# The routing table and row fetch of the next expert, moved in front of the down products of the expert before

## The chip, the cores and the metric

One core of a Trainium2 chip runs the whole program. The metric is the device time of one execution in microseconds (us), as the median of three runs.

## What is computed

One decoder layer over 512 tokens of width 2048: a mixer (pooling branch, forgetting attention, gates, output projection), then a mixture of 16 experts, then a last norm. Only the experts matter here:

```python
logits = h @ w_router                      # (512, 16)
# best group of 4 experts, then the 2 best experts in it: two experts per token, with weights
for each expert e, over the rows (at most 128 in a block) of the tokens that chose it:
    a, u = xb @ w_g[e], xb @ w_u[e]        # 2048 -> 1024 each
    y    = (silu(a) * u) @ w_d[e]          # 1024 -> 2048
    x[token] += gate_m * weight * y
```

All is float32. The kernel keeps that precision by splitting an operand into a high and a low part that TensorE reads at its fast rate (`chi` and `clo` of the weights, `xh` and `xl` of the rows, `glp` for both parts of the gated rows), and by adding three products: high by high, low by high, high by low.

## The kernel before

**Steps.** The expert stage is a list of items, one for each 128 rows of a weight matrix. Expert e has 16 gate-and-up steps `gu[e][0..15]` (`gu_item`, its 2048 columns are gate and up side by side) and 8 down steps `dn[e][0..7]` (`d_item`). A step is a load by SP, a split (ScalarE copies the high part, line 1132, then VectorE subtracts to get the low part, line 1133), and 12 matmuls of 512 columns (`rows3`, line 1147): three products into four PSUM banks. Even experts use banks 0 to 3 and odd ones banks 4 to 7 (`cset`).

**Order.** It is written out by hand. The first four gate-and-up steps of the next expert stand ahead of the down steps of an expert:

```python
NCR, LSC, LEAD = 8, 2, 4
c_items += nxt[:LEAD] + dn[e] + nxt[LEAD:]
```

So the list reads gu[e][0..3], dn[e-1][0..7], gu[e][4..15], gu[e+1][0..3], dn[e][0..7] and so on. Every engine works its own queue in this order. `run_items` (line 78) splits two items ahead of the matmuls (LSC), and there are LSC + 1 = 3 pairs of `chi` and `clo`, so the split of a step writes the pair that the step three places earlier has read. What is hung on an item by `.after` is written into the queues just ahead of the matmuls of the next item.

**Work hung on the steps.** After gu[e][15], `glu(e)`: ScalarE's silu (line 1250) and VectorE's product (line 1251) take the gate and up sums out of the four banks into `glr`. After gu[e+1][1], `glu_turn(e)`: TensorE turns these rows into the first two banks of the set (line 1262), and ScalarE and VectorE take them out as `glp` (lines 1267, 1268). After dn[e][7], `put_out(e)`: VectorE scales the down sums into `y` (line 1275, one instruction for each bank), and POOL adds `y` to the rows of the output by an indirect DMA (line 1280).

**Routing of the next expert.** `slot_hits(e)` (line 1575, VectorE) makes a one-hot tile that says which token sits in which of the 128 slots. It lies in the tile `G`. `table(e)` (line 1578) multiplies it on TensorE with a small list (line 1581: four matmuls of 8 columns into one bank), and three short VectorE instructions (lines 1584, 1585, 1588) read that bank and give the token numbers `dest` and the scales `tab`. `gather(e)` (line 1213, POOL) then fetches the expert's rows from DRAM (`zrows`) by an indirect DMA into `G`. `prep_rows` (line 1223, VectorE) scales `G` in four quarters after gu[e-1][9] to gu[e-1][11], and `prep_turn` turns it on TensorE (line 1238) and splits it into `xh` and `xl` (lines 1243, 1244).

Before the change, for expert e+1, the one-hot tile is made after dn[e-1][4], and the table and the fetch follow gu[e][5], which is the second gate-and-up step behind the down steps of expert e-1. The table's bank is the second of the set of expert e+1, which is also the set of e-1.

Of the kernel before, what the change touches and what calls it, by code (L numbers as in the profile page):

```python
# [138 lines left out]
def trunk_kernel(ctx: ExitStack, tc: tile.TileContext, x, c, w_ada, b_ada, norm_mix, norm_moe, w_in,  # L139
# [88 lines left out]
    def bank(i):  # L228
        return psB.tile([P, 512], F32, name=f"bank{i}", tag=f"bank{i}")
# [341 lines left out]
    for g in range(2, 8):  # L571
        n = f"A{g+1}" if g < 7 else "S0"
# [526 lines left out]
    NCR, LSC, LEAD = 8, 2, 4  # L1099
# [7 lines left out]
    def c_tile(name, shape, dt=F32, bufs=1):  # L1107
        return c_["left"].tile(shape, dt, name=name, tag=name, bufs=bufs)
# [102 lines left out]
    def slot_rows(tensor, e, to):  # L1211

        gp.indirect_dma_start(out=to, out_offset=None, in_=tensor[:],
                              in_offset=bass.IndirectOffsetOnAxis(ap=r_["dest"][:, e:e + 1], axis=0),
                              bounds_check=T - 1, oob_is_err=False)

    def gather(e):
        g = got[e] = xs[e] = c_tile("G", [P, D]) if e else xs[0]
        slot_rows(zrows, e, g)
# [118 lines left out]
    gu = {e: [gu_item(e, k) for k in range(KD)] for e in range(E)}  # L1338
    dn = {e: [d_item(e, k) for k in range(8)] for e in range(E)}
# [53 lines left out]
    def rtile(name, n=NBE, dt=F32, bufs=1):  # L1393
        return rt.tile([P, n], dt, name=name, tag=name, bufs=bufs)

    def b_e(t):
        return t.rearrange("p (b e) -> p b e", e=E)
# [7 lines left out]
    vv = v4.rearrange("p (b e c) -> p b e c", e=E, c=4)  # L1405
# [144 lines left out]
    vb = wr.rearrange("p k e -> p (k e)").bitcast(BF16).rearrange("p (b e c) -> p b e c", e=E, c=8)  # L1550
# [15 lines left out]
    ohs = {}  # L1566

    def slot_hits(e):

        oh = rtile("oh", NB * P) if e < 2 else c_tile("G", [P, D])[:, 0:NB * P]  # L1570
        if e:
            oh = oh.bitcast(BF16)[:, 0:NB * P]
        ohs[e] = oh = oh.rearrange("p (b s) -> p b s", b=NB)
        slot, pos = (slotb, posb) if e else (slot1, posm)
        dve.tensor_tensor(oh, slot[:, None, :].to_broadcast([P, NB, P]),
                          b_e(pos)[:, :, e:e + 1].to_broadcast([P, NB, P]), ALU.is_equal)

    def table(e):
        ps, oh, v, n = bank(4 * (e % 2) + 1), ohs.pop(e), vb if e else vv, 8 if e else 4
        for b in range(NB):  # L1580
            pe.matmul(ps[:, 0:n], lhsT=oh[:, b, :], rhs=v[:, b, e, :], start=b == 0, stop=b == NB - 1)
        if e:

            dve.tensor_reduce(at_[:, 0:1], ps[:, 0:2], axis=AX.X, op=ALU.add)
            dve.tensor_reduce(tab[:, e, :], ps[:, 2:8].rearrange("p (c i) -> p c i", i=3), axis=AX.X, op=ALU.add)
        else:
            dve.tensor_copy(tab[:, e, :], ps[:, 1:3])
        dve.tensor_scalar(dest[:, e:e + 1], at_[:, 0:1] if e else ps[:, 0:1], float(T), None, op0=ALU.add)
# [81 lines left out]
    slot_hits(0)  # L1670
    filled()
    table(0)
    gather(0)
    placed()
# [12 lines left out]
    c_items[1:1] = [Item(None, prep_first)]  # L1687
    c_items.insert(5, Item(gu[0][0].raw))
    for e in range(E - 1):
        (dn[e - 1][4] if e else gu[0][2]).after.append(lambda e=e: slot_hits(e + 1))  # L1690
        gu[e][LEAD + 1].after.append(lambda e=e: table(e + 1))
        gu[e][LEAD + 1].after.append(lambda e=e: gather(e + 1))
        for q in range(4):
            gu[e][NORM[q]].after.append(lambda e=e, q=q: prep_rows(e + 1, got[e + 1], q))
            gu[e][TURN[q]].after.append(lambda e=e, q=q: prep_turn(e + 1, q))
# [31 lines left out]
```

## Time and profile before

| | us |
|---|---|
| median of 3 runs | 2397.55 (2397.06 to 2399.11) |
| the profiled execution, its own time | 2397.21 |
| its span in the trace | 2395.5 |
| TensorE busy in the span | 2325.1 (97%) |
| VectorE busy in the span | 1748.3 (73%) |
| ScalarE busy in the span | 1163.7 (49%) |

The expert stage fills the second half of the span, from about 1250 us on. The sections on rows below are read like this: a row of a timeline gives the start, the duration (of all instructions of the row), the engine, the line, the operation with what it writes and reads, and in brackets how long the engine had been idle just before and what ended that. TensorE's matmuls overlap, so the distance from one start to the next is what a matmul costs, and it is shorter than the duration shown.

### The profile page before, as it was taken

What the parts mean: (1) busy time and instruction counts of PE and PEld (TensorE: products, weight loads), DVE (VectorE), ACT (ScalarE), POOL (GpSimd) and SP (SyncE); (2) the same over time, 40 slices, a digit from 0 to 9 for tenths busy, and PEclk for the clock granted to TensorE, in tenths of its full rate; (3) what the DMA queues carried; (4) which work ended last, traced back from release to release, by engine and by line L of the source; (5) the groups of instructions that cost most, each with busy time, mean ns of one, the idle gap of its engine ahead of it and who ended that gap; (6) DMA issues with size and microseconds to landing.
All of it is one profiled execution on the core that took longest, in us unless ns stands there. A gap on an engine that the chain in (4) does not pass through costs nothing.

```text
span 2395.5 us, 29296 instructions
## 1 busy us (share of the span) xinstructions
PE 2325.1 (97%) x11478; PEld 1929.4 (81%) x11478; DVE 1748.3 (73%) x1750; ACT 1163.7 (49%) x1070; POOL 127.7 (5%) x73
## 2 busy tenths in 40 slices
PE   7999999999999999999969999999999999999996
PEld 6888777788887888899968888888788888888883
DVE  7987333377665666343349999999999999999995
ACT  4323323322222222233227777777776777777775
POOL 0000100000000000000000111001101100100010
PEclk9999999999999999999979999999999999999998
DMA  9878724266665667366648999999998999999996
GB/s 338 277 245 205 101 71 71 71 234 240 237 233 192 236 233 256 108 201 196 222 152 314 347 372 384 399 384 368 371 381 345 376 411 366 372 378 376 376 359 264
DMA packets 269775, 662.57 MB, mean 277 GB/s; under 512 B 20084, under 2 KB 160620, under 8 KB 249708
## 3 DMA queue, kind: packets, MB, share of 16 engines
q1 hardware_dynamic: 262112, 641.89, 73.6%
q0 software_dynamic: 4752, 17.48, 3.0%
q8 instruction: 91, 1.49, 0.2%
q10 hardware_dynamic: 2768, 1.29, 0.2%
q14 instruction: 52, 0.43, 0.0%
HBM read 648.32 MB, written 29.39 MB: 283 GB/s over the span
## 4 chain that ended last, share of the span: by engine, by line
PE 77%; DMA 11%; DVE 7%; issue 3%; ACT 2%; POOL 0%; SPq 0%; POOLq 0%; DVEq 0%; ACTq 0%
PE bank L1147 27%; PE bank L242 10%; PE bank L244 10%; PE bank L243 10%; DMA G<-zrows,dest 4%; DVE clo L1133 3%; PE bank L645 3%; PE bank L647 3%; PE bank L648 3%; DMA craw<-in_w_exp_gate_dram 2%; DMA craw<-in_w_exp_down_dram 2%; DVE y L1275 1%; PE bank L1238 1%; ACT chi L1132 1%; PE bank L386 1%
## 5 line engine op out<-in xcount | busy, mean ns | idle before, releaser
L1133 DVE TENSOR_TENSOR clo<-craw,chi 128x2048 fp32r<-128x2048 f32 x270 | 615.7, 2289 | 53.4 <-ACT chi L1132 51.1
L1132 ACT ACTIVATE chi<-craw 128x2048 fp32r<-128x2048 f32 x270 | 518.0, 1920 | 218.3 <-PE bank L1147 202.2
L238 DVE TENSOR_TENSOR wlo<-raw,whi 128x1024 fp32r<-128x1024 f32 (+2 forms) x180 | 213.3, 1185 | 421.4 <-ACT whi L237 387.5
L237 ACT ACTIVATE whi<-raw 128x1024 fp32r<-128x1024 f32 (+2 forms) x180 | 184.6, 1027 | 653.6 <-PE bank L243 356.3
L242 PE MATMUL bank<-hh,whi 128*128 128x512 f32 x846 | 335.5, 397 | 1.4 <-ACT hh L406 1.3
L244 PE MATMUL bank<-hh,wlo 128*128 128x512 f32 x846 | 330.8, 391 | 1.6 <-DVE wlo L238 1.6
L243 PE MATMUL bank<-hl,whi 128*128 128x512 f32 x846 | 330.3, 390 | 0.3 <-DVE hl L410 0.3
L1147 PE MATMUL bank<-chi,xh 128*128 128x512 f32 x1020 | 288.4, 397 | 0.0
L1147 PE MATMUL bank<-clo,xh 128*128 128x512 f32 x1020 | 280.9, 389 | 0.1
L1147 PE MATMUL bank<-chi,xl 128*128 128x512 f32 x1020 | 280.7, 389 | 0.0
L1147 PE MATMUL bank<-chi,glp 128*128 128x512 f32 x992 | 255.4, 389 | 0.3 <-DVE glp L1268 0.3
L1147 PEld LDWEIGHTS bank<-clo,xh 128*128 128x128 f32 x1020 | 191.4, 188 | 41.1 <-DVE clo L1133 0.5
L1147 PEld LDWEIGHTS bank<-chi,xl 128*128 128x128 f32 x1020 | 191.5, 188 | 40.3
L1147 PEld LDWEIGHTS bank<-chi,glp 128*128 128x128 f32 x992 | 186.1, 188 | 39.6 <-DVE glp L1268 0.9
L1147 PEld LDWEIGHTS bank<-chi,xh 128*128 128x128 f32 x1020 | 185.7, 188 | 34.4
L244 PEld LDWEIGHTS bank<-hh,wlo 128*128 128x128 f32 x846 | 159.2, 188 | 36.7 <-DVE wlo L238 3.1
L242 PEld LDWEIGHTS bank<-hh,whi 128*128 128x128 f32 x846 | 159.4, 188 | 35.3 <-ACT hh L406 1.5
L243 PEld LDWEIGHTS bank<-hl,whi 128*128 128x128 f32 x846 | 159.4, 188 | 33.4 <-issue 1.0
L906 DVE SCALAR_TENSOR_TENSOR acc<-raw,cact,acc 128x1024 f32<-128x1024 f32 x120 | 154.0, 1283 | 11.1 <-DMA raw<-in_w_ada_dram 8.5
L645 PE MATMUL bank<-whi,hh 128*128 128x256 f32 x512 | 146.0, 285 | 0.0
L647 PE MATMUL bank<-wlo,hh 128*128 128x256 f32 x512 | 144.8, 283 | 0.0
L648 PE MATMUL bank<-whi,hl 128*128 128x256 f32 x512 | 144.8, 283 | 0.0
(393 smaller groups left out, 3218.5 us busy)
## 6 DMA issues: line engine op xcount, KB each, us to landing
craw<-in_w_exp_down_dram SPq DMA_DIRECT2D x114, 1024.0 KB, 13.3
raw<-in_w_ada_dram SPq DMA_DIRECT2D x82, 1024.0 KB, 6.1
craw<-in_w_exp_gate_dram SPq DMA_DIRECT2D x161, 512.0 KB, 9.9
craw<-in_w_exp_up_dram SPq DMA_DIRECT2D x161, 512.0 KB, 10.0
raw<-in_w_gate_dram SPq DMA_DIRECT2D x32, 1024.0 KB, 5.7
raw<-in_w_branch_dram SPq DMA_DIRECT2D x16, 1024.0 KB, 5.0
raw<-in_w_out_dram SPq DMA_DIRECT2D x16, 1024.0 KB, 9.3
raw<-in_w_in_dram SPq DMA_DIRECT2D x14, 1024.0 KB, 10.7
```

What stands on the lines that cost most here:

```text
L237: act.activation(hi[:, :n], raw[:, :n], AF.Copy)
L238: dve.tensor_tensor(lo[:, :n], raw[:, :n], hi[:, :n].bitcast(F32), ALU.subtract)
L242: pe.matmul(o, lhsT=whi, rhs=xhi, start=first, stop=False)
L243: pe.matmul(o, lhsT=whi, rhs=xlo, start=False, stop=False)
L244: pe.matmul(o, lhsT=wlo, rhs=xhi, start=False, stop=last)
L645: pe.matmul(o, lhsT=sh, rhs=hi[:, js], start=k + kk == 0 and b % 2 == 0, stop=False, skip_group_check=True)
L647: pe.matmul(o, lhsT=sh, rhs=lo[:, js], start=False, stop=False, skip_group_check=True)
L648: pe.matmul(o, lhsT=sl, rhs=hi[:, js], start=False, stop=k + kk == nk - 1, skip_group_check=True)
L906: dve.scalar_tensor_tensor(cell["a"], r, s, cell["a"], op0=ALU.mult, op1=ALU.add)
L1132: act.activation(hi, raw, AF.Copy)
L1133: dve.tensor_tensor(lo, raw, hi.bitcast(F32), ALU.subtract)
L1147: pe.matmul(ps.tiles[n], lhsT=rows, rhs=w[:, n * 512:(n + 1) * 512], start=first and i == 0, stop=last and i == 2)
```

## The change

For every expert from the third on (e+1 with e from 1 to 14), the table and the fetch now follow gu[e][2], so they stand ahead of gu[e][3] and of the eight down steps of expert e-1, eleven items earlier. The one-hot tile follows gu[e-1][15], right behind `glu`, nine items earlier. The table's bank is the fourth of its set and no longer the second, since `glu_turn` uses the first two at that place. For the second expert (e = 0) place and order stay; only the bank is another.

```diff
-        ps, oh, v, n = bank(4 * (e % 2) + 1), ohs.pop(e), vb if e else vv, 8 if e else 4
+        ps, oh, v, n = bank(4 * (e % 2) + 3), ohs.pop(e), vb if e else vv, 8 if e else 4
...
     for e in range(E - 1):
-        (dn[e - 1][4] if e else gu[0][2]).after.append(lambda e=e: slot_hits(e + 1))
-        gu[e][LEAD + 1].after.append(lambda e=e: table(e + 1))
-        gu[e][LEAD + 1].after.append(lambda e=e: gather(e + 1))
+
+        (gu[e - 1][15] if e else gu[0][2]).after.append(lambda e=e: slot_hits(e + 1))
+        at_step = gu[e][LEAD - 2 if e else LEAD + 1].after
+        at_step += [lambda e=e: table(e + 1), lambda e=e: gather(e + 1)]
```

What this does to the queues is shown for one expert in the middle of the stage. Its gate-and-up steps use banks 0 to 3, and the down steps of the expert before use banks 4 to 7.

**Place 1, TensorE, where the down steps begin.** Before, the last high-by-low product of gu[e][3] (`xl`) is followed by the first product of dn[e-1][0] (`glp`); a wait in brackets names the engine waited for:

```order
L1147 MATMUL bank3_12044<-chi1_12063,xl0_11938 128x512
L1147 MATMUL bank4_12141<-chi2_12081,glp_12089 128x512 [waits DVE_49]
L1147 MATMUL bank5_12142<-chi2_12081,glp_12089 128x512 [waits DVE_49]
L1147 MATMUL bank6_12143<-chi2_12081,glp_12089 128x512
L1147 MATMUL bank7_12144<-chi2_12081,glp_12089 128x512
L1147 MATMUL bank4_12141<-clo2_12082,glp_12089 128x512
```

Now the table stands one step earlier on TensorE, between gu[e][2] and gu[e][3], and writes bank 7:

```order
L1147 MATMUL bank3_12046<-chi0_12032,xl0_11938 128x512
L1581 LDWEIGHTS G_12041 [waits DVE_49]
L1581 MATMUL bank7_12125<-wr_82,G_12041 128x8
L1581 LDWEIGHTS G_12041
L1581 MATMUL bank7_12125<-wr_82,G_12041 128x8
L1581 LDWEIGHTS G_12041
L1581 MATMUL bank7_12125<-wr_82,G_12041 128x8
L1581 LDWEIGHTS G_12041
L1581 MATMUL bank7_12125<-wr_82,G_12041 128x8
L1147 MATMUL bank0_12043<-chi1_12065,xh0_11937 128x512 [waits Activation_49]
```

After the 12 matmuls of gu[e][3], dn[e-1][0] begins as before, but its matmul into bank 7 has waits of its own:

```order
L1147 MATMUL bank3_12046<-chi1_12065,xl0_11938 128x512
L1147 MATMUL bank4_12155<-chi2_12083,glp_12091 128x512 [waits DVE_49]
L1147 MATMUL bank5_12156<-chi2_12083,glp_12091 128x512 [waits DVE_49]
L1147 MATMUL bank6_12157<-chi2_12083,glp_12091 128x512
L1147 MATMUL bank7_12158<-chi2_12083,glp_12091 128x512 [waits DVE_49,PE_49]
L1147 MATMUL bank4_12155<-clo2_12084,glp_12091 128x512
```

What moved: the table's four matmuls came in front of gu[e][3], and the fourth matmul of the first down step, which waited for nothing new before, now waits for VectorE and for TensorE's own table in the same bank.

**Place 2, VectorE, at the same place of the program.** Before, between `glu` (`glr`) and the second down step; `clo1` with `craw2` belongs to gu[e][3], `clo2` with `craw3` to dn[e-1][0], `clo0` with `craw0` to dn[e-1][1]:

```order
L1251 TENSOR_TENSOR glr_12036<-bank7_11527,glr_12036 128x512 [waits PE_49,Activation_49]
L1133 TENSOR_TENSOR clo1_12064<-craw2_7013,chi1_12063 128x2048 [waits DMAHW2_49,DMAHW1_49,Activation_49]
L1133 TENSOR_TENSOR clo2_12082<-craw3_7195,chi2_12081 128x2048 [waits DMAHW3_49,Activation_49]
L1268 TENSOR_TENSOR glp_12089<-bank4_12085,glp_12089 128x512 [waits Activation_49]
L1268 TENSOR_TENSOR glp_12089<-bank5_12086,glp_12089 128x512 [waits Activation_49]
L1133 TENSOR_TENSOR clo0_12120<-craw0_6635,chi0_12119 128x2048 [waits DMAHW4_49,Activation_49]
L1133 TENSOR_TENSOR clo1_12138<-craw4_7394,chi1_12137 128x2048 [waits DMAHW5_49,Activation_49]
```

Now:

```order
L1251 TENSOR_TENSOR glr_12036<-bank7_11529,glr_12036 128x512 [waits PE_49,Activation_49]
L1575 TENSOR_TENSOR G_12041<-bT_75,cntw_83 128x512
L1133 TENSOR_TENSOR clo1_12066<-craw2_7013,chi1_12065 128x2048 [waits DMAHW2_49,DMAHW1_49,Activation_49]
L1133 TENSOR_TENSOR clo2_12084<-craw3_7195,chi2_12083 128x2048 [waits DMAHW3_49,Activation_49]
L1268 TENSOR_TENSOR glp_12091<-bank4_12087,glp_12091 128x512 [waits Activation_49]
L1268 TENSOR_TENSOR glp_12091<-bank5_12088,glp_12091 128x512 [waits Activation_49]
L1133 TENSOR_TENSOR clo0_12122<-craw0_6635,chi0_12121 128x2048 [waits DMAHW4_49,Activation_49]
L1584 TENSOR_REDUCE cntw_83<-bank7_12125 128x1 [waits PE_49]
L1585 TENSOR_REDUCE tab_8533<-bank7_12125 128x2
L1588 TENSOR_SCALAR dest_8534<-cntw_83 128x1 [waits DVE_49]
L1133 TENSOR_TENSOR clo1_12152<-craw4_7394,chi1_12151 128x2048 [waits DMAHW5_49,Activation_49]
```

What moved: the one-hot instruction (line 1575) came in behind `glr`, and the three table instructions came in behind the low part of the second down step.

**Place 3, TensorE, where the table stood.** Before, between gu[e][5] and gu[e][6], into the bank that VectorE's second `y` instruction had to leave first:

```order
L1147 MATMUL bank3_12044<-chi2_12268,xl0_11938 128x512
L1581 LDWEIGHTS G_12236
L1581 MATMUL bank5_12336<-wr_82,G_12236 128x8 [waits DVE_49]
L1581 LDWEIGHTS G_12236
L1581 MATMUL bank5_12336<-wr_82,G_12236 128x8
L1581 LDWEIGHTS G_12236
L1581 MATMUL bank5_12336<-wr_82,G_12236 128x8
L1581 LDWEIGHTS G_12236
L1581 MATMUL bank5_12336<-wr_82,G_12236 128x8
L1147 MATMUL bank0_12041<-chi0_12284,xh0_11937 128x512 [waits Activation_49]
```

Now the steps follow each other there:

```order
L1147 MATMUL bank3_12046<-chi2_12280,xl0_11938 128x512
L1147 MATMUL bank0_12043<-chi0_12296,xh0_11937 128x512 [waits Activation_49]
L1147 MATMUL bank2_12045<-chi0_12296,xh0_11937 128x512
L1147 MATMUL bank1_12044<-chi0_12296,xh0_11937 128x512
L1147 MATMUL bank3_12046<-chi0_12296,xh0_11937 128x512
```

What moved: the four table matmuls and their wait for VectorE are gone from here. On POOL the fetch of expert e+1 is now issued ahead of the scatter of expert e-1, and before it was issued behind it. SP's queue has the same loads in the same order.

## Rows read from the trace of the kernel before

**Rows 1.** The page's busy times (engine, busy us and share, instructions) and its chain that ended last by engine.

```profile
PE 2325.1 (97%) x11478; PEld 1929.4 (81%) x11478; DVE 1748.3 (73%) x1750; ACT 1163.7 (49%) x1070; POOL 127.7 (5%) x73
...
PE 77%; DMA 11%; DVE 7%; issue 3%; ACT 2%; POOL 0%; SPq 0%; POOLq 0%; DVEq 0%; ACTq 0%
```

**Rows 2.** The windows view of the stretch of the middle experts: its length, then busy us (and instructions) of PE, PEld, DVE, ACT and POOL, then TensorE's granted clock, the share of the DMA engines, and GB/s.

```profile
1344.00:2248.00 904.00, 893.59 (x4113) 734.15 (x4113) 842.92 (x574) 648.47 (x417) 89.74 (x26) 1.00 0.95 376
```

**Rows 3.** The waits of TensorE from 1300 to 2330 us, all of them: who waited for whom, us in total, times, longest.

```profile
PE bank L1238 <- DVE G L1223: 7.4, 10, 1.5
PE bank L1581 <- DVE y L1275: 3.0, 14, 0.2
```

**Rows 4.** TensorE's timeline: tables (line 1581) of the first, two following and the last of the 14 experts from the third on, and the first turn of `G` (line 1238) behind each of the two in the middle.

```profile
1344.39 0.24 PE L1581 MATMUL bank<-wr,G 128*128 128x8 bf16 x4 [0.22 <-DVE y L1275]
...
1623.29 0.24 PE L1581 MATMUL bank<-wr,G 128*128 128x8 bf16 x4 [0.22 <-DVE y L1275]
1639.82 0.60 PE L1238 MATMUL bank<-ident,G 128*128 128x128 f32 x4
1691.92 0.24 PE L1581 MATMUL bank<-wr,G 128*128 128x8 bf16 x4 [0.21 <-DVE y L1275]
1710.12 0.66 PE L1238 MATMUL bank<-ident,G 128*128 128x128 f32 x4 [1.51 <-DVE G L1223]
...
2247.92 0.24 PE L1581 MATMUL bank<-wr,G 128*128 128x8 bf16 x4 [0.21 <-DVE y L1275]
```

**Rows 5.** TensorE's timeline, the start of the step ahead of a table and of the step behind it: first for the table of the second expert, then for one of those with the wait.

```profile
1272.79 1.07 PE L1147 MATMUL bank<-chi,xh 128*128 128x512 f32 x4
1275.63 1.16 PE L1147 MATMUL bank<-chi,xh 128*128 128x512 f32 x4
...
1688.83 1.07 PE L1147 MATMUL bank<-chi,xh 128*128 128x512 f32 x4
1692.02 1.17 PE L1147 MATMUL bank<-chi,xh 128*128 128x512 f32 x4
```

**Rows 6.** TensorE's timeline where the down steps begin: the first matmuls of dn[e-1][0] (`glp`) for the first two of the 14 experts, for one in the middle with gu[e][3] ahead of it, and for the last of the 14.

```profile
1316.57 1.29 PE L1147 MATMUL bank<-chi,glp 128*128 128x512 f32 x4
...
1386.46 1.07 PE L1147 MATMUL bank<-chi,glp 128*128 128x512 f32 x4
...
1661.63 1.07 PE L1147 MATMUL bank<-chi,xh 128*128 128x512 f32 x4
1664.35 1.07 PE L1147 MATMUL bank<-chi,glp 128*128 128x512 f32 x4
1665.25 1.07 PE L1147 MATMUL bank<-clo,glp 128*128 128x512 f32 x4
...
2220.35 1.07 PE L1147 MATMUL bank<-chi,glp 128*128 128x512 f32 x4
```

**Rows 7.** VectorE's timeline at the same four places. In the middle: `glr`, the low parts of gu[e][3] and dn[e-1][0] in one row, `glp`, the low part of dn[e-1][1]. The other rows are the low part of dn[e-1][1] of the other three.

```profile
1316.76 2.28 DVE L1133 TENSOR_TENSOR clo<-nf,chi 128x2048 fp32r<-128x2048 f32 x1
...
1385.97 2.28 DVE L1133 TENSOR_TENSOR clo<-nf,chi 128x2048 fp32r<-128x2048 f32 x1
...
1656.99 1.28 DVE L1251 TENSOR_TENSOR glr<-bank,glr 128x512 f32<-128x512 f32 x2
1658.18 4.48 DVE L1133 TENSOR_TENSOR clo<-craw,chi 128x2048 fp32r<-128x2048 f32 x2
1662.59 1.28 DVE L1268 TENSOR_TENSOR glp<-bank,glp 128x512 fp32r<-128x512 f32 x2
1663.79 2.29 DVE L1133 TENSOR_TENSOR clo<-craw,chi 128x2048 fp32r<-128x2048 f32 x1
...
2219.78 2.28 DVE L1133 TENSOR_TENSOR clo<-craw,chi 128x2048 fp32r<-128x2048 f32 x1
```

**Rows 8.** VectorE's timeline: a low part with two table instructions behind it, and a one-hot instruction with the low part behind it.

```profile
1626.66 2.29 DVE L1133 TENSOR_TENSOR clo<-craw,chi 128x2048 fp32r<-128x2048 f32 x1
1628.87 0.15 DVE L1584 TENSOR_REDUCE cntw<-bank 128x1 f32<-128x2 f32 x1
1628.93 0.15 DVE L1585 TENSOR_REDUCE tab<-bank 128x2 f32<-128x6 f32 x1
...
1682.31 0.68 DVE L1575 TENSOR_TENSOR G<-bT,cntw 128x512 bf16<-128x512 bf16 x1
1682.91 2.29 DVE L1133 TENSOR_TENSOR clo<-xh,chi 128x2048 fp32r<-128x2048 f32 x1
```

**Rows 9.** ScalarE's timeline: the high part of dn[e-1][1] at the middle place of Rows 6 and 7.

```profile
1661.83 1.92 ACT L1132 ACTIVATE chi<-craw 128x2048 fp32r<-128x2048 f32 x1 [0.72 <-PE bank L1147]
```

**Rows 10.** POOL's timeline at one expert, a scatter and the fetch behind it, and VectorE's first instruction on the fetched rows.

```profile
1693.47 5.58 POOL L1280 DMA_INDIRECT acc<-y,dest  x1 [61.09 <-DVE y L1275]
1699.35 1.66 POOL L1213 DMA_INDIRECT G<-zrows,dest  x1 [0.31 <-issue]
...
1709.32 0.75 DVE L1223 SCALAR_TENSOR_TENSOR G<-G,tab,shrow 128x512 f32<-128x512 f32 x1 [1.85 <-DMA G<-zrows,dest]
```

**Rows 11.** The page's queue of software DMAs (packets, MB, share of 16 engines), and the two longest waits of SP's queue from 1345 to 2250 us.

```profile
q0 software_dynamic: 4752, 17.48, 3.0%
...
SPq L1154 <- DMA acc<-y,dest: 195.0, 14, 15.0
SPq L1185 <- DVE clo L1133: 162.3, 54, 5.8
```

## The prediction

> **What bounds the kernel now.** I read the page first, for the engine that sets the end: TensorE is busy 97% of the span, and 77% of the chain that ended last runs over it [rows 1]. Then the windows view of the expert stage: in 904.0 us TensorE is busy 893.6 us at a granted clock of 1.00, which is its upper level of 2.4 GHz [rows 2]. Third, what TensorE waits for there: two things, and the change touches both, the rows `G` of the next expert (10 waits, 7.4 us) and, ahead of the table, VectorE's `y` (14 waits, 3.0 us) [rows 3]. Last, the timelines, since these lists count idle time from the end of a matmul, while the next one starts before that end. I price by starts.
>
> From table to table is one expert. Thirteen of them take 2247.92 - 1344.39 = 903.53 us, 69.50 each [rows 4]. One without a wait for `G` takes 1691.92 - 1623.29 = 68.63 us [rows 4]. In it the first turn of `G` starts 16.53 us behind the table; in the next one, with a listed wait of 1.51 us, it starts 18.20 us behind, 1.67 us more [rows 4]. The rows are late because of POOL's order: the scatter is issued at 1693.47, the fetch only behind it at 1699.35, and VectorE stands idle for 1.85 us until the rows land [rows 10].
>
> **What the change takes away.** *The wait for `G`.* The fetch is now issued about eleven steps earlier, at 2.72 us a step (1664.35 - 1661.63) [rows 6] some 30 us. The longest loss seen is under 2 us, so I take it as gone: 13 x (69.50 - 68.63) = **11.3 us**. Its low end is the listed 7.4 us [rows 3].
>
> *The table's wait for `y`.* The table of the second expert, which does not wait, costs 1275.63 - 1272.79 - 2.72 = 0.12 us; one that waits for `y` costs 1692.02 - 1688.83 - 2.72 = 0.47 us [rows 5]. At its new place its bank was emptied by `glu` before, and the one-hot tile is ready two steps ahead. So 14 x 0.35 = **4.9 us** go; low end the listed 3.0 [rows 3].
>
> Here a rule bears on the price. By the wait list the two gains are 10.4 us, by starts 16.2. The Trainium skill (Perfetto Trace Analysis, Tensor Engine Instruction) says that the end of a TensorE instruction in a profile is worked out from its size and not observed. By it the list, which rests on such ends, is no price, and the trace agrees: 1.67 us lost against 1.51 listed. With the list's values the sum below would be +13.7, with the starts it is +7.9.
>
> **What it adds.** The table now writes the fourth bank of the set that the down steps of expert e-1 fill next. The fourth matmul of the first down step can't start until VectorE has read the table out (lines 1584 and 1585), and on VectorE these two stand behind the low part of the *second* down step. So TensorE waits for work that it needs only a step later. For the expert in the middle:
>
> - TensorE reaches that matmul at 1664.35 + 0.12 (the table, now ahead of it) + 3 x 0.225 (four matmuls take 1665.25 - 1664.35) = 1665.15 [rows 5, 6].
> - VectorE runs without a gap from `glr` to the low part of dn[e-1][1], which starts at 1663.79 [rows 7]. The one-hot instruction now stands in this train and pushes it by 1682.91 - 1682.31 = 0.60 [rows 8]: 1664.39. Line 1585 starts 1628.93 - 1626.66 = 2.27 behind the start of the low part and takes 0.15 [rows 8], so it ends at 1666.81. From the end of a VectorE instruction to TensorE's start I take 0.05 (1709.32 + 0.75 to 1710.12) [rows 4, 10]: 1666.86.
> - The wait is 1666.86 - 1665.15 = 1.71 us.
>
> The last of the 14 reads alike: the low part starts 0.57 us ahead of the first `glp` matmul, against 0.56 in the middle; the second has 0.49 [rows 6, 7]. Only the first differs, it starts 0.19 us behind [rows 6, 7]; the same sum gives 2.46 us with the push and 1.86 without; I take 1.86. Together 13 x 1.71 + 1.86 = **24.1 us**. Nothing covers it: apart from the two waits above TensorE waits for nothing in this stage, and behind the place it goes on step by step.
>
> Low end: the one-hot's 0.60 us cost nothing. Then 1.11 us stay, since ScalarE starts the high part of dn[e-1][1] at 1661.83, when TensorE has left that buffer, and ends at 1663.75, 0.04 ahead of the low part [rows 7, 9]. 14 x 1.11 = 15.5. High end: all at the second expert's distance (0.07 more), and release only after the third table instruction (line 1588, at most 0.15 more): 14 x 1.93 = 27.0.
>
> **Small moves.** The one-hot leaves the down steps and the three table instructions leave gu[e][5], where VectorE has slack: it is busy 843 of 904 us [rows 2]. The low parts of gu[e][3] and dn[e-1][0] now end at 1661.1 and 1663.3, still 1.6 and 2.1 us ahead of the matmuls that read them [rows 6, 7]; `glp` ends at 1664.47, and its second half is needed at 1664.70. On POOL the fetch goes ahead of the scatter: 30 us apart, neither holds the other up. SP's loads keep their order. I cost these at nothing.
>
> **Sum.** 24.1 - 11.3 - 4.9 = +7.9 us on the profiled execution's 2397.2, that is **2405.1 us**; the median shown is 0.35 above that execution. With 0.2% (4.8 us) as what a measurement of this kernel can tell from no change, this is slower. Ends: 15.5 - 16.2 = -0.7 (2396.5) and 27.0 - 10.4 = +16.6 (2413.8).
>
> **The rivals.**
> 1. *Faster: TensorE does not wait at the fourth matmul.* If VectorE ran far enough ahead there, only the gains stay: 2397.2 - 16.2 = 2381. It decides at (16.2 - 4.8) / 14 = 0.81 us of wait: below that the change is faster. For it: VectorE loses its idle time for `G`, 1.85 us in one expert [rows 10]. Against it: the high part on ScalarE can't start before TensorE has left the buffer [rows 9], which alone gives 1.11. Chance 0.08.
> 2. *No change: the one-hot's push is swallowed.* The low end above, 2396.5. Against it: VectorE shows no gap there [rows 7]. Chance 0.08.
> 3. *No change: the weight loads set the pace.* The DMA engines are 0.95 busy at 376 GB/s [rows 2]. Then moving waits about on TensorE gives 2397. Against it: TensorE waits for no load there [rows 3], and SP's queue waits 162.3 us for tiles that VectorE has yet to free [rows 11], so loads are ahead of their use. The Trainium skill (HBM Reference, Specifications) gives about 358 GB/s for each core; by that the stage's 340 MB would take an estimated 949 us, and the trace ran it in 904, so that figure does not bind here. Chance 0.10.
> 4. *Much slower: the fetch comes between the weight loads.* Queue 0 moved 17.48 MB [rows 11] in 33 transfers (16 fetches, 15 scatters and two at the end of the program), 0.53 MB each, 1.41 us at 376 GB/s [rows 2]. If the loads were late by that each time: 14 x 1.41 = 20 more, 2425. Against it: the same queue of SP as in 3, and its 14 stops of up to 15.0 us for the scatter [rows 11] that no step feels. Chance 0.06.
>
> That the change does not do what it says is no case: the order shows table, wait and fetch at the new places.
>
> **How the numbers follow.** The forecast, 2402 to 2414, has 0.68. With rival 4 slower has 0.74; rivals 2 and 3 make same 0.18; faster 0.08. The range goes from 2396 (rivals 2 and 3) to 2413, just under the high end, and leaves out rivals 1 and 4 and a little at its edges.
>
> **What would show it.** Table to table about 70.0 us (68.63 - 0.35 + 1.71) and nearly equal in all experts. Rows 3 replaced by one wait of TensorE's line 1147 for VectorE's table, 14 times, about 1.55 us each as listed. No wait for `G`, the table's start right behind its step, the fetch issued about 40 us ahead of its first reader. It is wrong if the fourth `glp` matmul follows the third without a gap, if the gap is near 1.1, or if loads show up as TensorE's waits.

## The result, and the profile after

| | before | after |
|---|---|---|
| median of the runs, us | 2397.31 (2396.65 to 2399.11, 4 runs) | 2412.37 (2410.29 to 2413.11, 4 runs) |
| ratio to before, with its 95% interval | | 1.0062 [1.0049, 1.0074] |
| span of the profiled execution, us | 2395.5 | 2411.4 |

The change makes the kernel slower by 15.1 us. The forecast was +7.9 (2405.1, range 2396 to 2413). A second comparison, on another chip, gave 2409.83 and 1.0072 [1.0055, 1.009]; it is told with the experiments.

The page of the changed kernel, busy times and the chain that ended last, as in [rows 1]:

```profile
PE 2326.1 (96%) x11478; PEld 1925.0 (80%) x11478; DVE 1747.1 (72%) x1750; ACT 1163.3 (48%) x1070; POOL 185.4 (8%) x73
...
PE 66%; DVE 16%; DMA 9%; issue 6%; ACT 3%; POOLq 0%; DVEq 0%; SPq 0%; ACTq 0%
```

TensorE does the same work in the same busy time. What is new is idle time between its instructions, and VectorE's share of the chain, which went from 7 to 16%. The windows view from the first to the last of the 14 tables (columns as in [rows 2]):

```profile
1312.38:2229.26 916.88, 895.43 (x4109) 732.37 (x4108) 841.36 (x573) 647.84 (x417) 140.83 (x26) 1.00 0.92 367
```

Thirteen experts take 916.88 us, 70.53 each, where before they took 69.50 [rows 4]. The clock is at its upper level, 1.00, in both. The loads run at 367 GB/s and no longer at 376, as about the same bytes (336 MB against 340) are spread over a longer time. POOL's row grew from 89.74 to 140.83 us; the last section comes back to it.

The wait lists of the changed kernel: TensorE's matmuls from 1300 to 2345 us, all of them (as [rows 3]), then two rows of its weight loads from 1345 to 2265 us.

```profile
PE bank L1147 <- DVE dest L1588: 21.5, 14, 1.6
...
PEld bank L1147 <- issue: 25.0, 13, 1.9
PEld bank L1147 <- DVE clo L1133: 6.9, 13, 0.5
```

Both lines of [rows 3] are gone. In their place stands one wait for the table, 14 times, 1.54 us each as listed. The first row of the weight loads is the same stop once more, seen from the load of the matmul that waits. The last row is easily passed over, since it stands with the weight loads: 13 times TensorE waits for a low part (`clo`), 0.53 us each. It turns out to be the point the prediction missed.

TensorE's timeline, in order of time: the first table; then one expert in the middle from the turn of `glr` on, through the table, gu[e][3] and the first down step; then the start of gu[e][4], and gu[e][7] with its three products; the first turn of `G`; the next turn of `glr` and the next table; and the last table. It answers to [rows 4 to 6].

```profile
1312.38 0.26 PE L1581 MATMUL bank<-wr,G 128*128 128x8 bf16 x4
...
1661.47 1.03 PE L1262 MATMUL bank<-ident,glr 128*128 128x128 f32 x8
...
1665.08 0.26 PE L1581 MATMUL bank<-wr,G 128*128 128x8 bf16 x4
1665.19 1.18 PE L1147 MATMUL bank<-chi,xh 128*128 128x512 f32 x4
...
1668.05 0.84 PE L1147 MATMUL bank<-chi,glp 128*128 128x512 f32 x3
1670.41 0.47 PE L1147 MATMUL bank<-chi,glp 128*128 128x512 f32 x1 [1.52 <-DVE dest L1588]
1670.72 1.09 PE L1147 MATMUL bank<-clo,glp 128*128 128x512 f32 x4
...
1691.60 1.07 PE L1147 MATMUL bank<-chi,xh 128*128 128x512 f32 x4
...
1699.76 1.07 PE L1147 MATMUL bank<-chi,xh 128*128 128x512 f32 x4
1700.93 1.20 PE L1147 MATMUL bank<-clo,xh 128*128 128x512 f32 x4
1701.96 1.07 PE L1147 MATMUL bank<-chi,xl 128*128 128x512 f32 x4
...
1713.76 0.60 PE L1238 MATMUL bank<-ident,G 128*128 128x128 f32 x4
...
1731.95 1.03 PE L1262 MATMUL bank<-ident,glr 128*128 128x128 f32 x8
1735.56 0.26 PE L1581 MATMUL bank<-wr,G 128*128 128x8 bf16 x4
...
2229.26 0.26 PE L1581 MATMUL bank<-wr,G 128*128 128x8 bf16 x4
```

Two things are to be seen. The first down step has three matmuls, then a hole: the fourth should start 3 x 0.225 behind the first, at 1668.73, and starts at 1670.41, **1.68 us** late. And in gu[e][7] the second product starts 1.17 us behind the first and the third 1.03 behind that, where a product takes 0.91 (four matmuls of some 0.225). The turn of `G` waits for nothing.

VectorE at the same place (as [rows 7, 8]), and then where gu[e][7] is prepared:

```profile
1661.62 0.70 DVE L1575 TENSOR_TENSOR G<-bT,cntw 128x512 bf16<-128x512 bf16 x1
1662.22 4.50 DVE L1133 TENSOR_TENSOR clo<-craw,chi 128x2048 fp32r<-128x2048 f32 x2
1666.63 1.30 DVE L1268 TENSOR_TENSOR glp<-bank,glp 128x512 fp32r<-128x512 f32 x2
1667.82 2.30 DVE L1133 TENSOR_TENSOR clo<-craw,chi 128x2048 fp32r<-128x2048 f32 x1
1670.02 0.17 DVE L1584 TENSOR_REDUCE cntw<-bank 128x1 f32<-128x2 f32 x1
1670.09 0.17 DVE L1585 TENSOR_REDUCE tab<-bank 128x2 f32<-128x6 f32 x1
1670.23 0.15 DVE L1588 TENSOR_SCALAR dest<-cntw 128x1 int32<-128x1 f32 x1
...
1695.96 2.72 DVE L1275 SCALAR_TENSOR_TENSOR y<-bank,tab,gmrow 128x512 f32<-128x512 f32 x4
1698.59 2.28 DVE L1133 TENSOR_TENSOR clo<-glr,chi 128x2048 fp32r<-128x2048 f32 x1
```

The table's sums were in the bank from about 1665.3 on. VectorE comes to them at 1670.02, behind the one-hot tile, two low parts, `glp` and the low part of the second down step. It ends line 1588 at 1670.38, and TensorE starts at 1670.41. (Only lines 1584 and 1585 read the bank, and they are done by 1670.26; why TensorE goes on only behind line 1588 was not tested.) Further down, the low part for gu[e][7] (its weights were loaded into the tile `glr`, which is free then) can start only when `y` is done, at 1698.59; it ends at 1700.87, and the product that reads it starts at 1700.93.

**Where the time went.** I cut each expert at four starts on TensorE's timeline, from one turn of `glr` to the next, and added up the 14 experts (us):

| | before | after | difference |
|---|---|---|---|
| turn of `glr` to the first down step (the table's new place) | 88.75 | 92.11 | +3.36 |
| the eight down steps | 304.88 | 330.01 | +25.13 |
| gu[e][4] to the first turn of `G` (the table's old place) | 321.84 | 310.52 | -11.32 |
| first turn of `G` to the next turn of `glr` | 257.13 | 254.73 | -2.40 |
| all | 972.60 | 987.37 | +14.77 |

That is the 15.1 us between the medians, to 0.3. In before, an expert without a wait for `G` takes 22.35 in the third row and 18.20 in the fourth, so these waits made 321.84 - 14 x 22.35 + 257.13 - 14 x 18.20 = 8.9 + 2.3 = 11.3 us. After, all 14 experts read nearly alike: 6.58, 23.56, 22.17 and 18.20, together 70.5.

### The profile page after: what moved, and what is told of

Read it like the earlier page. It is cut to its first block, busy times and chain, and to the rows that moved or that the text cites. A ratio compares the mean times of both kernels' runs of the same rounds, so it can differ in the third digit from the quotient of the medians.

```text
span 2411.4 us, 29297 instructions
## 1 busy us (share of the span) xinstructions
PE 2326.1 (96%) x11478; PEld 1925.0 (80%) x11478; DVE 1747.1 (72%) x1750; ACT 1163.3 (48%) x1070; POOL 185.4 (8%) x73
## 4 chain that ended last, share of the span: by engine, by line
PE 66%; DVE 16%; DMA 9%; issue 6%; ACT 3%; POOLq 0%; DVEq 0%; SPq 0%; ACTq 0%
PE bank L1147 19%; PE bank L244 10%; PE bank L242 10%; PE bank L243 10%; DVE clo L1133 9%; PE bank L645 3%; PE bank L647 3%; PE bank L648 3%; DMA craw<-in_w_exp_down_dram 2%; ACT chi L1132 2%; DMA craw<-in_w_exp_gate_dram 2%; DMA craw<-in_w_exp_up_dram 2%; DVE y L1275 1%; DMA raw<-in_w_gate_dram 1%; DVE G L1223 1%
## 5 line engine op out<-in xcount | busy, mean ns | idle before, releaser
L1147 PE MATMUL bank<-chi,glp 128*128 128x512 f32 x992 | 258.6, 390 | 22.4 <-DVE dest L1588 21.5
L1280 POOL DMA_INDIRECT acc<-y,dest x15 | 123.3, 8219 | 414.8 <-DVE y L1275 414.8
## 6 DMA issues: line engine op xcount, KB each, us to landing
raw<-in_w_in_dram SPq DMA_DIRECT2D x14, 1024.0 KB, 10.4
```

The lines of the kernel that those rows point to most:

```text
L1147: pe.matmul(ps.tiles[n], lhsT=rows, rhs=w[:, n * 512:(n + 1) * 512], start=first and i == 0, stop=last and i == 2)
L1280: gp.indirect_dma_start(out=acc[:], out_offset=bass.IndirectOffsetOnAxis(ap=r_["dest"][:, e:e + 1], axis=0), in_=weigh(e), in_offset=None, ...
```

## The experiments

The theories that the expectations speak of: **A**, the prediction's own, is that the loss is the table's bank, which VectorE empties late because the table instructions stand behind the low part of the second down step. Its rival **B** is that the early fetch or the moved one-hot slows the down steps, and the table's wait only shows it. **G** is on the waits for `G` in the kernel before: that they come from the fetch standing behind the scatter on POOL. Kernels compared on one chip share the runs of before there. These lie between 2385 and 2398 us (one to ten waits for `G` were seen in kernels that leave the fetch at its old place), so each kernel has its own ratio. The names in brackets are those that the expectations may use.

**1. The table one step earlier still (e1).** In the change:

```diff
-        at_step = gu[e][LEAD - 2 if e else LEAD + 1].after
+        at_step = gu[e][LEAD - 3 if e else LEAD + 1].after
```

Expected: 

> The change with table and fetch one step earlier still, behind gu[e][1] and the turn of glr, so that the three table instructions stand ahead of the low part of dn[e-1][1] on VectorE. Theory A (the loss is TensorE waiting at the fourth matmul of the first down step, 1.68 us and 0.11 us of refill, 14 times): the wait vanishes, VectorE leaves the bank at about the time glp ends plus 0.36, some 0.4 us ahead of the fourth matmul. 2412.4 - 14 x 1.79 = 2387.3, plus up to 0.1 us each where the table waits for the one-hot tile (1.4): 2387 to 2389, faster than before by 8 to 10. Theory B (the early fetch, with POOL busy 185 us instead of 128 and the scatter landing after 16.9 us instead of 12.5, slows loads and the stage): the fetch is as early here, so the time stays within 5 us of 2412, or falls by less than half of 25.

Measured: 2386.05 (2383.51 to 2390.0) against 2390.0 for before, ratio 0.9987 [0.9975, 0.9999]. TensorE's timeline of this kernel, the first two products of the first down step and the start of gu[e][4]:

```profile
1659.10 1.07 PE L1147 MATMUL bank<-chi,glp 128*128 128x512 f32 x4
1660.00 1.07 PE L1147 MATMUL bank<-clo,glp 128*128 128x512 f32 x4
...
1680.86 1.07 PE L1147 MATMUL bank<-chi,xh 128*128 128x512 f32 x4
```

The hole is gone, and the eight steps take 21.76 us, as before. In the sum of the 14 experts the down steps went from 330.01 to 304.67 and nothing else moved by over 0.2 us. Fetch and one-hot are at least as early here, and the down steps take no longer for it. A holds, B falls. It also says that the change's whole loss hung on one step's place. The time is a little below the 2387 to 2389 that were expected, but it is 4 us faster than before and not 8 to 10, since before itself takes 2390 on this chip and not 2397.

**2. The first down step bank by bank (e2).** The table stays where the change put it, but the first down step does all three products of one bank before the next, so the table's bank comes up at the tenth matmul and not at the fourth:

```diff
-    def rows3(ps, sh, sl, hi, lo, first, last, order=(0, 1, 2, 3)):
+    def rows3(ps, sh, sl, hi, lo, first, last, order=(0, 1, 2, 3), by_bank=False):
...
-        steps = [(n, i) for n in order for i in range(3)] if last else [(n, i) for i in range(3) for n in order]
+        steps = [(n, i) for n in order for i in range(3)] if last or by_bank else [(n, i) for i in range(3) for n in order]
...
-            rows3(sets[e], gh[:, k, :], gl[:, k, :], *cell.pop("w"), k == 0, k == 7)
+            rows3(sets[e], gh[:, k, :], gl[:, k, :], *cell.pop("w"), k == 0, k == 7, by_bank=k == 0)
```

Expected: 

> The change as it is, but the first down step of each expert runs its 12 matmuls bank by bank, so that the table's bank comes as the 10th matmul and not as the 4th. No instruction is added or moved on another engine. Theory A: TensorE comes to that bank 6 x 0.227 = 1.36 us later, so of the wait of 1.68 us some 0.32 stay: 2412.4 - 14 x 1.36 = 2393.3 (2391 to 2395). Theory B: nothing moves on the queues of DMAs, 2412.

Measured: 2392.68 (2389.23 to 2395.11), ratio 1.0013 [1.0002, 1.0025]. TensorE's waits:

```profile
PE bank L1147 <- DVE dest L1588: 2.1, 12, 0.3
```

The time is in the expected range. The down steps take 310.96 us, 6.1 over those of before, 0.44 an expert where 0.32 was expected: a hole of 0.31 (1663.63 + 0.23 to 1664.17 in its timeline), and again some 0.12 behind it. Six matmuls of 0.225 us put between the table and its reader (1.35 us) took 1.36 out of the 1.80: the loss is a distance in time.

**3. The one-hot tile alone (e5).** In the kernel before, only the one-hot tile goes to its new place:

```diff
-            (dn[e - 1][4] if e else gu[0][2]).after.append(lambda e=e: slot_hits(e + 1))
+            (gu[e - 1][15] if e else gu[0][2]).after.append(lambda e=e: slot_hits(e + 1))
```

Expected: 

> The kernel before with only the one-hot tile moved, behind gu[e-1][15]; table, bank and fetch as before. It adds 0.60 us to VectorE's train between glr and the low part of dn[e-1][1] and takes them out of the down steps. Theory A: no one waits for that train closely without the table, so 2397.3 within 2. Rival (VectorE's train is itself what TensorE waits for, and the table's bank only shows it): up to 14 x 0.6 = 8 more, 2405.

Measured: 2394.1 (2391.38 to 2396.53) against 2391.05, ratio 1.0012 [1.0002, 1.0023]. The weight loads' waits of this kernel:

```profile
PEld bank L1147 <- DVE glp L1268: 3.3, 14, 0.4
```

That is 3.0 us above before on this chip, so neither within A's 2 us nor near the rival's 8. The 0.60 us that the one-hot pushes VectorE's train cost 0.10 us an expert, 306.23 - 304.88 = 1.4 us in the down steps: `glp` comes late for the first of them. The rest is not accounted for. The prediction priced the push at nothing. In the changed kernel no wait for `glp` is listed; there the table in front holds TensorE back by 0.24 us at this place.

**4. The fetch alone left behind (e4).** In the change, the table stays at its new place and the fetch goes back to its old one, behind the scatter:

```diff
-        at_step += [lambda e=e: table(e + 1), lambda e=e: gather(e + 1)]
+        at_step.append(lambda e=e: table(e + 1))
+        gu[e][LEAD + 1].after.append(lambda e=e: gather(e + 1))
```

Expected: 

> The change with one-hot tile and table early, but the fetch left where it was, behind gu[e][5] and the scatter. Theory A: the wait at the fourth matmul stays, the wait for G comes back with its 0.87 us an expert, and the new wait for the low part behind y (0.39 us each) stays, since it has nothing to do with the fetch: 2412.4 + 11 = 2423 (2419 to 2426). Theory B (the early fetch costs the 7 us that were not forecast): 2412.4 + 11 - 7 = 2416 or less, and no wait behind y.

Measured: 2433.98 (2428.89 to 2447.19), ratio 1.0201 [1.0168, 1.0234], so 11 us above what was expected. TensorE's waits, and then two scatters on POOL with the fetch behind each:

```profile
PE bank L1147 <- DVE dest L1588: 21.3, 14, 1.6
PE bank L1238 <- DVE G L1223: 14.9, 3, 5.7
```

```profile
1488.69 9.97 POOL L1280 DMA_INDIRECT acc<-y,dest  x1 [65.48 <-DVE y L1275]
1498.96 1.71 POOL L1213 DMA_INDIRECT G<-zrows,dest  x1 [0.31 <-issue]
...
1567.59 3.37 POOL L1280 DMA_INDIRECT acc<-y,dest  x1 [66.91 <-DVE y L1275]
1571.27 1.35 POOL L1213 DMA_INDIRECT G<-zrows,dest  x1 [0.31 <-issue]
```

The wait for the table is the same 1.5 us without the early fetch, and the wait behind `y` stays (7.4 us of waits for a low part, 14 times), a second time against B. The miss is in the other row: not ten waits for `G` of under 2 us, but three of about 5 us, in just the three experts whose scatter held POOL for 10 us instead of 3.4. Against the changed kernel they cost 15.2 us ahead of the first turn of `G` and 6.5 behind it, and the early fetch of the change avoids that.

**5. The table in another bank, at its old place (e3).** In the kernel before:

```diff
-        ps, oh, v, n = bank(4 * (e % 2) + 1), ohs.pop(e), vb if e else vv, 8 if e else 4
+        ps, oh, v, n = bank(4 * (e % 2)), ohs.pop(e), vb if e else vv, 8 if e else 4
```

The table's bank is now the one that the first `y` instruction empties and no longer the second. Expected: 

> The kernel before with only the table's bank changed, the first of its set and not the second, which VectorE's y leaves 0.66 us sooner. Theory A (what the table's wait for y held back is needed soon after: the low part of gu[e][7] stands behind the four y instructions on VectorE, and would be only 0.32 us ahead of TensorE in the trace of before): the wait of 0.35 us at the table goes, and the low part of gu[e][7] is then just in time: 2397.3 - 14 x 0.32 = 2392.8 (2392 to 2394). Rival (that wait costs nothing, since the steps behind it are bound otherwise): 2397.3.

Measured: 2383.49 (2380.21 to 2386.8), ratio 0.9973 [0.9962, 0.9984], 6.5 us below before. Its waits, TensorE's matmuls and weight loads:

```profile
PE bank L1238 <- DVE G L1223: 1.7, 1, 1.7
...
PEld bank L1147 <- DVE clo L1133: 3.9, 14, 0.3
```

The table's wait for `y` is gone, as expected, but the segment gu[e][4] to `G` went only from 22.35 to 22.17 us, 0.18 and not 0.32: the low part of gu[e][7] now comes just in time (a wait of 0.3 for it is listed), and the four matmuls that read it take 1.04 us and not 0.91. It is the same wait as in the changed kernel. So 2.5 of the 6.5 us are the table's. The other 4 are probably waits for `G`, of which only one is left in this trace; before was not profiled on this chip, so that is not shown, and why they would go stays open. Both theories, which took before at 2397.3, missed the time.

**6. `y` in two halves (e6).** This tests that new wait. Experiment 1's place of the table, and VectorE makes two of the four `y` instructions behind dn[e][7] and the other two, with the scatter, behind gu[e+1][4], so the low part of gu[e][7] no longer stands behind all four:

```diff
-            dn[e][7].after.append(lambda e=e: put_out(e))
+            dn[e][7].after.append(lambda e=e: weigh(e, (0, 1)))
+            nxt[LEAD].after.append(lambda e=e: put_out(e))
```

(`weigh` now takes a list of quarters, and `put_out` weighs quarters 2 and 3 itself. In this kernel the fetch for the last norm stands ahead of the last such scatter, so the rows there lack expert 14's part.) Expected: 

> The first experiment (table and fetch behind gu[e][1]) with put_out in two halves: two y instructions behind dn[e][7], two and the scatter one step later, so that a low part stands between them on VectorE. Theory A: the wait for the low part of gu[e][7] behind four y instructions (0.27 us and 0.12 us of refill, 14 times) goes as well: 14 x 0.39 = 5.5 below the first experiment, about 2382 to 2384. Rival (that wait only moves to the next low part, since VectorE has the same work in the same time): no change against the first experiment. Risk: the scatter and with it SP's next load into y come 2.7 us later.

Measured: 2382.53 (2378.14 to 2383.09) against 2391.05, ratio 0.9963 [0.995, 0.9976]. The segment from gu[e][4] to `G` is 304.78 / 14 = 21.77 us, 0.40 below the changed kernel's. Eight steps at 2.72 are 21.76, so nothing is left in it. By the ratios (0.9963 against 0.9987) that is 5.7 us below experiment 1, where 5.5 were expected.

**7. The same, with the last fetch behind the last scatter (e7).** The whole layer is computed:

```diff
-    dn[14][7].after.append(gather_last)
+    gu[15][LEAD].after.append(gather_last)
```

Expected: 

> The sixth experiment (table and fetch behind gu[e][1], y in two halves) with the fetch for the last norm behind the last scatter, as in the kernel before; in the sixth it stood ahead of it. Theory A: nothing but the end of the program moves, so the sixth's 2382.5 within 4, 0.996 of before; an expert takes 68.3 us from turn to turn of glr.

Measured: 2385.42 (2383.59 to 2387.36) against 2393.35, ratio **0.9965 [0.9952, 0.9977]**: 7.9 us faster than the kernel before, and faster than the change by some 24. TensorE's timeline: gu[e][4], gu[e][7] with its second product, and the first turn of `G`:

```profile
1681.41 1.07 PE L1147 MATMUL bank<-chi,xh 128*128 128x512 f32 x4
...
1689.57 1.07 PE L1147 MATMUL bank<-chi,xh 128*128 128x512 f32 x4
1690.47 1.07 PE L1147 MATMUL bank<-clo,xh 128*128 128x512 f32 x4
...
1703.17 0.60 PE L1238 MATMUL bank<-ident,G 128*128 128x128 f32 x4
```

The second product of gu[e][7] now follows the first at 0.90 us, where the changed kernel had 1.17, and from gu[e][4] to `G` it is 21.76. An expert takes 68.6 us from turn to turn of `glr`, 0.3 more than expected. Some of the gain is lost again behind that, up to the next turn of `glr`: TensorE waits three times, 3.0 us in all, for `glr`.

**8. Before and after once more (e8, e9).** Both kernels unchanged, on the chip of experiment 7. Expected: 

> The kernel before, unchanged, for its trace and times on this chip. Theory G: the wait for G depends on how long the scatter holds POOL (3.38, 5.58 or 9.98 us in the traces so far); an expert has the wait only where the scatter took 5.58 or more, at 0.6 to 1.9 us each, so the kernel before takes 2385 to 2386 with few such experts and 2397 with ten. Rival: the wait follows the chip's memory speed, with no tie to the scatter's time on POOL.

 and 

> The change, unchanged, on this chip. Theory A with G: its stall at the fourth matmul and its wait behind y don't depend on the scatter, and it has no wait for G, so 2412 within 2 and a spread below that of before; where before takes 2390, the ratio is 1.009.

Measured: before 2391.99 (2389.17 to 2397.04), 0.9995 [0.9986, 1.0005]; after 2409.83 (2408.5 to 2413.9), 1.0072 [1.0055, 1.009], 0.2 us outside what was expected. In the changed kernel the experts take 70.5 us each again, with 21.4 us of waits for the table. In before, the waits for `G` (8.4 us, 10 times, in the profiled run, the slowest of its runs) can be set beside its scatters, of which these are two:

```profile
1483.55 5.57 POOL L1280 DMA_INDIRECT acc<-y,dest  x1 [61.72 <-DVE y L1275]
...
1693.72 3.38 POOL L1280 DMA_INDIRECT acc<-y,dest  x1 [61.11 <-DVE y L1275]
```

Nine experts have a scatter of 5.58 us, and there gu[e][4] to `G` takes 23.36 on average; five have one of 3.38, and there it takes 22.54. That speaks for a tie, but G as it was put is false: one expert with 5.58 has 22.35, no wait at all, and two with 3.38 have 22.75 and 22.81, a wait of 0.4 and more.

**9. The fetch ahead of the scatter, nothing else (e10).** In the kernel before, `y` is made as before, but its scatter is issued behind the fetch (the tile `y` is lent to SP's loads one step later for that):

```diff
-            dn[e][7].after.append(lambda e=e: put_out(e))
+            dn[e][7].after.append(lambda e=e: ys.update({e: weigh(e)}))
...
             gu[e][LEAD + 1].after.append(lambda e=e: gather(e + 1))
+            if e:
+                gu[e][LEAD + 1].after.append(lambda e=e: put_out(e - 1, ys.pop(e - 1)))
```

Expected: 

> The kernel before with only POOL's order turned: the scatter of expert e-1 is issued behind the fetch of expert e+1, both behind gu[e][5], and y's tile is lent to SP one step later. Table, one-hot and bank as before. Theory G: the fetch no longer stands behind the scatter, so the wait for G (11.3 us in the profile of before) goes in every expert and the stage takes 68.6 an expert: 2385 to 2387, whatever the chip. Rival (the fetch is late because its own descriptors or the memory are slow): the waits stay and 2390 or more; SP's load into y comes some 6 us later, which could cost up to that once in each expert if the loads are short of slack.

Measured: 2393.61 (2389.68 to 2396.16), ratio 1.0001 [0.9992, 1.001], as the rival has it. TensorE's waits (the table's matmul stands on line 1585 of this kernel):

```profile
PE bank L1238 <- DVE G L1223: 4.9, 8, 1.2
PE bank L1585 <- DVE y L1275: 3.0, 14, 0.2
```

Eight waits for `G` are left with no scatter ahead of the fetch, so G falls. The traces show why the order on POOL matters so little. In every one of the 14 experts of before, of experiments 3, 5 and 8 and of this one, the fetch's instruction on POOL ends 14.9 us behind the start of gu[e][4], whether a scatter of 5.6 us, one of 3.4 or none stands ahead of it. What differs is when the rows land, 3.8 to 8.6 us behind that, and the first reader is ready for them after 6.4. Behind a scatter of 5.6 us they mostly land later (20.7 to 23.5 us behind gu[e][4]) than behind one of 3.4 (18.7 to 22.0); what makes the landing long or short stays open. Only a scatter of 10 us, in experiment 4, holds the fetch itself back. The old place is too tight for the fetch: it takes 6.8 to 10.4 us from issue to landing in this kernel, and between the table's `dest` and the first reader of the rows lie some 9.5 us.

## Why the prediction was right or wrong

**The number.** The forecast was +7.9 us and +15.1 came, 0.6 us inside the range. Direction and main cause were right, but that the range held is luck: its high end, +16.6, was made of a longer stall (27.0) and of gains at the listed prices (10.4). The stall came to 25.1, and the gains did come to 10.4, but as 11.3 from `G` less 0.9 from a term that the prediction had as a gain of 3.0 at the least. The wait list's sum, +13.7, lies nearer than +7.9 by the same luck.

**The stall at the fourth matmul: right in mechanism, 1.0 us short.** Forecast 24.1 us, measured 25.1 (1.80 an expert). 1.68 us is the hole itself, against 1.71 forecast. The first sum took line 1585 as the releaser and 0.05 us behind it; the trace shows line 1588 and 0.03, which stood in the high end. The other 0.12 us comes behind the hole: the next matmul starts 0.31 us behind the released one and not 0.225. That was not in the sum. That 1.68 lies so near 1.71 is luck in part: TensorE came to the place 0.12 us later than forecast, behind the table, and VectorE let the bank go 0.14 later (2.56 us behind the start of the low part and not 2.42), and the two nearly cancel. The list of waits says 1.54 us each (21.5 / 14) where the starts say 1.68 for the hole and 1.80 in all, the point that the Trainium skill makes on estimated ends (Perfetto Trace Analysis, Tensor Engine Instruction); the trace agrees again, and by the list this term would have been 3.6 us short.

**The wait for `G`: right in size, not in its reason.** Forecast -11.3 us, found 11.3 us in before and none after. The prediction said that the rows are late because the fetch stands behind the scatter on POOL. Experiment 9 and the traces show that, with scatters of 3.4 and 5.6 us, this order does not delay the fetch's instruction at all; the old place is too close to the first reader for the time that the rows take to land.

**The table's wait for `y`: this term failed.** The prediction put it at -4.9 us: 0.35 an expert for the wait, with the table itself at 0.12 in either place. Measured: leaving the old place gave 22.35 - 22.17 = 0.18 an expert, and arriving at the new one cost 0.24 (3.36 / 14): together **+0.9 us**. The old place without a table would be eight clean steps, 21.76, so 0.59 did leave. Less the 0.24 at the new place that is the 0.35 of the forecast: a table without a wait costs 0.24 and not 0.12, as the step behind it is slower too, but it does so at either place. But 0.41 came in. TensorE reaches gu[e][7] 0.59 us sooner, and the low part that it reads there stands behind the four `y` instructions on VectorE. In before the same place reads, on VectorE and then on TensorE:

```profile
1690.46 2.72 DVE L1275 SCALAR_TENSOR_TENSOR y<-bank,tab,gmrow 128x512 f32<-128x512 f32 x4
1693.10 2.28 DVE L1133 TENSOR_TENSOR clo<-glr,chi 128x2048 fp32r<-128x2048 f32 x1
...
1694.85 1.07 PE L1147 MATMUL bank<-chi,xh 128*128 128x512 f32 x4
1695.76 1.07 PE L1147 MATMUL bank<-clo,xh 128*128 128x512 f32 x4
```

The low part ends at 1695.38; with the 0.06 us from its end to TensorE's start that the changed kernel shows (1700.87 to 1700.93), its reader could have started at 1695.44, and it starts at 1695.76. So the low part was 0.32 us ahead, 0.27 are missing now, and that is the hole: 1.17 - 0.90. With the 0.12 by which the product behind it is slower (1.03 and not 0.91) this makes 0.39. The table's wait had covered a second wait for the same work. Experiments 6 and 7 show it: with `y` in halves the segment takes 21.76 to 21.77. This is 5.8 of the 6.9 us by which the sum was short, and the stall's 1.0 the rest. The prediction did not ask what is late next where the wait goes: its check of low parts covered gu[e][3] and dn[e-1][0] alone.

**Small moves at nothing.** Nearly right: the one-hot costs 0.10 us an expert where it stands alone (experiment 3). The loads pace nothing, and no wait for a load appears.

**The rivals.** 1 (no wait at the fourth matmul) is false by the timeline. 2 (the push is swallowed) would have left a hole of 1.11 and not 1.68. 3 (loads pace) falls with the 14.8 us that the stage grew at a lower DMA share. 4 (the fetch between the loads) falls with experiment 1, whose fetch is at least as early and whose down steps are as short as those of before. The case forecast, slower by the table's bank, is shown, by experiments 1 and 2.

**What was to be seen.** Table to table 70.0 was forecast, 70.53 came; nearly equal experts, one listed wait of about 1.55 us for the table 14 times, and no wait for `G` came as said.

## What to carry to other kernels

When a few columns borrow a PSUM bank, the price is set by when the in-order engine that empties it gets there, not by how short its instructions are: look up what stands ahead of the reader in its queue, and give the bank that much distance (here one step of 2.7 us turned +0.6% into -0.1%). When a wait is taken away, go forward on the waiting engine until it has made up the whole gain, and ask at each step whether its operands are ready that much sooner; a second wait for the same work often lies under the first. Read the list of the weight loads' waits too: such a wait may stand only there.

## What the runs showed that was not expected

- The scatter of a block holds POOL for very different times, about 3.4, 5.6, 7.8 or 10 us in the twelve traces (and 2.4 in experiment 9, where it starts at another moment), for the same work: that of the third of the 14 experts took 5.57 us in before, 9.98 in the changed kernel and 3.37 in experiment 3. In the changed kernel most are of the longest kind, and POOL's busy time went from 127.7 to 185.4 us. POOL's timeline of the changed kernel, a fetch and two scatters:

```profile
1671.14 2.38 POOL L1213 DMA_INDIRECT G<-zrows,dest  x1 [32.72 <-issue]
1698.96 3.37 POOL L1280 DMA_INDIRECT acc<-y,dest  x1 [25.44 <-DVE y L1275]
1769.47 9.98 POOL L1280 DMA_INDIRECT acc<-y,dest  x1 [25.46 <-DVE y L1275]
```

  The steps between them are 2.2 us, the distance of two low parts that follow each other on VectorE (1698.59 to 1700.79). In all twelve traces every scatter of the stage ends 1.4 to 1.5 us behind the end of a low part (line 1133), the first to fourth that ends while it runs, and every fetch 0.9 us behind the end of the first. The scatter of 1698.96 above ends at 1702.33, 1.46 us behind the low part that ends at 1700.87. So POOL seems to get on only when VectorE ends a low part; no experiment changed that, and which low part ends the scatter stays open. The Trainium skill (SBUF — State Buffer, Who interferes with whom) says that a VectorE instruction with two inputs in SBUF contends with a GpSimd instruction that reads SBUF; a low part has two such inputs and the ends fit, but no run here shows that this is the cause. It costs the change nothing, as its fetch is 28 us ahead of the scatter, and the scatters of 10 us are what made experiment 4 so slow.
- A full step of matmuls right behind the table's four small ones takes 2.86 us and not 2.72 (1665.19 to 1668.05 in the changed kernel), with its first four taking 1.02 instead of 0.91. So the table costs 0.11 us up to the next start and some 0.13 behind it, and a price taken up to the next start alone misses half.
- The kernel before is itself uneven: on the three chips of the experiments its runs lie between 2385 and 2398 us, and its two profiled runs, both near 2397, have ten late fetches each. The changed kernel's experts are even, and slower.
